# Differential attention with RG-LRU on one core: negated scaled scores, value scale in a copy, products re-placed

## The chip, the core and the metric

One core of a Trainium2 chip runs the kernel. The metric is device time in microseconds (us), the median of three runs: 497.36 us before (497.15 to 498.44). One further execution was taken with a profile. The engines have short names: PE (TensorE), DVE (VectorE), ACT (ScalarE), POOL (GpSimd), and SP, which issues most DMAs.

## The reference

A hybrid encoder layer on 16 meta rows and 1024 sequence rows of width 1024. One projection gives queries, keys, values, a gate and the two inputs of a linear recurrence (RG-LRU). The part that the change touches is differential attention: four heads, each with two score maps whose softmaxes are subtracted.

```
scores = einsum('bqhmd,bkhmd->bhmqk', qb, kb) * scale
scores = where(mask, scores, -inf)          # chunk-causal, 64 rows a chunk
p = softmax(scores, axis=-1)
w = p[:, :, 0] - lam * p[:, :, 1]
o = einsum('bhqk,bkhd->bqhd', w, vb)
...
o = rms_norm(o, subln_w, SUBLN_EPS) * (1.0 - lam_init)
att_out = o * silu(g_att)
lru_out = rg_lru(conv(x_lru)) * silu(g_lru)
out = rms_norm(h + concat(att_out, lru_out) @ w_out, final_norm_w)[16:]
```

## The kernel before

Nearly all products are split into a high and a low half and done as three passes. The first part (up to about 250 us) projects the sequence, gate by gate, and runs the recurrence on the other engines. What follows, from the first score to the end, is the attention with everything that can be pushed beneath it; the change lies there.

**Tiles and steps.** The 1024 query rows make eight tiles of 128, worked in the order 3, 7, 6, 5, 4, 2, 1, 0 (tile i sees the first 16 + 128(i+1) keys, so the work of a step differs). `order` has 32 steps, one for each tile and head. `attend()` writes the instructions of a step in program order:

1. `transposes` of the weights of the step three back (PE into PSUM, ACT copies out as `wT`);
2. `scores(i, h, 0)`, the first map;
3. waiting products (`at_least`) up to two thirds of the step's number in the table `MF`, with `combine` of the step before between them;
4. `transposes` of the low half, then `scores(i, h, 1)`, the second map, then the rest of the step's `MF` products;
5. `halve` of the step before, and `weigh`: the product with the values (`O`) of the step three back.

The "waiting products" are a list (`fill`): first the value projection (`psv`), then for each tile the product of the recurrence's result with the output weights (`psol`, four pieces of six matmuls a tile), later that of the attention's result (`psoa`). `MF[s]` says how many pieces step s places; a piece is six 512-wide matmuls. Its sum is 88.

**One map** (`scores`). PE writes scores into `pss`. DVE adds the mask and takes the row maximum in one instruction (a custom operation and a short read of its accumulator, which gives `mx`). For tile 7, whose row is longer than 1024, the 16 meta columns are kept apart (`sme`, `m2`), so DVE also takes the larger of `mx` and `m2`, a `TENSOR_TENSOR` of 128x1. ACT then makes the bias from the maximum, `mx*nesc + lnsw` (an `Identity` of 128x1), and next `Exp(esc*e + mx)` over the row with its sum. `esc` is the score scale of each row, `nesc` its negative; both are 128x1 operands.

**combine and halve.** DVE forms the ratio of the two sums (`rec`, then a `TENSOR_SCALAR` into `mx`), joins the two maps (`SCALAR_TENSOR_TENSOR e<-e,mx`), and splits the result into two fp16 halves (`w`). ACT does the first half for tiles 7 and 3. POOL copies the meta columns aside (`wm`).

**finish** (a chain of small steps for each tile, taken up whenever the planner's clock has moved on): ACT copies `O` to `o`, DVE scales `rec` by `isc[:, 2:3]` (the value scale), ACT squares and sums `o` by head (`sq`), DVE and POOL make the inverse root (`sums`, a power on POOL), POOL multiplies `o` by the gate and by `rec`, and PE transposes `o` (`pa`) once the planner believes `o` to be ready. ACT copies `pa` to `af`, POOL splits that into `at`, and the tile's `psoa` pieces join the list.

**The planner.** `Clock` keeps a made-up time for each engine from a fixed cost per instruction; `tick` and `pace` hand out the background chains by it, so a change of a cost or of an instruction list moves where chains are written into the program. Among those chains is `load_wo`, which loads rows of the output weights (`woraw`, SP), copies the high half on ACT (`woh`) and subtracts on POOL (`wol`, 128x1024).

PSUM holds two score banks of 1024 columns (later narrower ones), three banks shared by products and transposes (`bank`), and one for `O`; a product waits until DVE or ACT has emptied the bank that it takes. Each engine's queue runs in order: an instruction that waits holds back all that stand behind it.

Of the kernel before, what the change touches and what calls it, by code (L numbers as in the profile page):

```python
# [12 lines left out]
AF = mybir.ActivationFunctionType  # L13
OP = mybir.AluOpType
AX = mybir.AxisListType
# [4 lines left out]
T = NM + S  # L20
# [10 lines left out]
NEG = -3.0e38  # L31
# [6 lines left out]
class Clock:  # L38
# [5 lines left out]
    def __init__(self):  # L44
        self.now = dict.fromkeys(self.RATE, 0.0)
        self.written, self.used, self.rings = {}, {}, {}

    def ready(self, *aps):
        return max([self.written.get(a.tensor.name, 0.0) for a in aps], default=0.0) + self.HOP
# [11 lines left out]
    def engine(self, key, eng):  # L61
        clock = self

        class Timed:
            def __getattr__(self, op):
                f = getattr(eng, op)

                def call(*a, **k):
                    aps = [x for x in list(a) + list(k.values()) if hasattr(x, "tensor")]
                    clock.step(key, op, aps)  # L70
                    return f(*a, **k)  # L71
                return call
        return Timed()

    def step(self, key, op, aps):
        fix, rate = self.RATE[key]
        out = aps[0]
        n = int(np.prod(out.shape[1:]))
        if key == "PE" and aps[-1].dtype == F32 and op == "matmul":
            rate *= 4  # L80
        if op == "tensor_copy" and key == "V":
            rate *= 0.55
        t = max(self.now[key], self.ready(*aps) if key != "PE" else
                max(self.written.get(x.tensor.name, 0.0) for x in aps))
        t += fix + n * rate
        self.now[key] = t
        for x in aps:
            self.used[x.tensor.name] = t
        self.written[out.tensor.name] = t
# [3 lines left out]
def hybrid_layer_kernel(ctx: ExitStack, tc: tile.TileContext, xT, x, meta, w6, nwT,  # L93
                        par, wg, lamv, subw, w_out, fnw, cosT, sinT, ident, sel, bmask, out):
    nc = tc.nc
    clock = Clock()
    V, A, G, PE = (clock.engine(k, e) for k, e in zip(("V", "A", "G", "PE"),
                                                      (nc.vector, nc.scalar, nc.gpsimd, nc.tensor)))
# [210 lines left out]
    for k in range(KC - 2):  # L309
# [16 lines left out]
        if k == 3:  # L326
# [20 lines left out]
            e = cst([P, NB], name="spe")  # L347
# [62 lines left out]
    lnsw = cst([P, 1], name="lnsw")  # L410
# [51 lines left out]
    mask = cst([P, T], BF16, name="mask")  # L462
# [3 lines left out]
    isc = cst([P, 3], name="isc")  # L466
# [315 lines left out]
    esc = cst([P, 1], name="esc")  # L782
# [70 lines left out]
    def begin(i):  # L853
        n = NM + P * (i + 1)
        d = st[i] = dict(n=n, k0=NM if n > 1024 else 0,
                         sm=cst([P, 2, NH], name=f"sums{i}"), mx=cst([P, 2, NH], name=f"mx{i}"),
                         rec=cst([P, 2, NH], name=f"rec{i}"),
                         wm=const.tile([P, 2, NH, NM], F16, tag="wm", bufs=3, name="wm"),
                         e={}, w={}, wT={})
        if d["k0"]:  # L860
            pm = bank([P, NMAP, NM], name="pssm")
            q = QT[i]
            for m in range(NMAP):
                PE.matmul(pm[:, m, :], q[:, 0, m, :], K[m][:, 0:NM], start=True, stop=False)
                PE.matmul(pm[:, m, :], q[:, 1, m, :], K[m][:, 0:NM], start=False, stop=True)
            sme = slot("raw", [P, NMAP, NM], name="sme")
            V.tensor_copy(sme, pm)
            m2 = cst([P, NMAP], name="m2")
            V.tensor_reduce(m2, sme, axis=AX.X, op=OP.max)
            d["sme"], d["m2"] = sme, m2  # L870

    def scores(i, h, a):

        d = st[i]
        n, k0, q, m = d["n"], d["k0"], QT[i], 2 * h + a
        ps = score_banks()
        for j in range(2):
            for s0 in range(0, n - k0, 512):
                s1 = min(s0 + 512, n - k0)
                PE.matmul(ps[:, s0:s1], q[:, j, m, :], K[m][:, k0 + s0:k0 + s1], start=(j == 0), stop=(j == 1))  # L880
        e = slot("work", [P, T], name="e")
        mx = d["mx"][:, a, h:h + 1]
        V.tensor_tensor_reduce(out=e[:, k0:n], in0=ps[:, 0:n - k0], in1=mask[:, T - n + k0:],
                               op0=OP.add, op1=OP.max, scale=1.0, scalar=NEG, accum_out=mx)
        if k0:
            A.copy(e[:, 0:NM], d["sme"][:, m, :])
            V.tensor_tensor(mx, mx, d["m2"][:, m:m + 1], op=OP.max)
        A.activation(mx, mx, AF.Identity, scale=nesc, bias=lnsw)
        A.activation(e[:, 0:n], e[:, 0:n], AF.Exp, scale=esc, bias=mx, accum_out=d["sm"][:, a, h:h + 1])
        d["e"][h, a] = e  # L890

    def combine(i, h):
# [65 lines left out]
    def finish(i):  # L958

        d = st[i]  # L960
        O = d["O"]
        r0 = d["rec"][:, 0, :]
        V.tensor_scalar(r0, r0, isc[:, 2:3], None, op0=OP.mult)
        g = slot("raw", [P, NH, P], name="gate")
        dma(g, ga_d[i].rearrange("p (h d) -> p h d", h=NH))
        o = slot("raw", [P, NH, P], name="o")
        A.copy(o.rearrange("p h d -> p (h d)"), O)
        yield
        so = d["sm"][:, 0, :]
        sq = const.tile([P, P], BF16, tag="sq", bufs=1, name="sq")  # L970
        for h in range(NH):
            A.activation(sq, o[:, h, :], AF.Square, scale=r0[:, h:h + 1], accum_out=so[:, h:h + 1])
        yield
        yield
        V.tensor_scalar(so, so, 1.0 / P, SUBLN_EPS, op0=OP.mult, op1=OP.add)
        G.tensor_tensor(so, so, pw[:, 0:NH], op=OP.pow)
        yield
        yield
        G.tensor_tensor(r0, r0, so, op=OP.mult)
        G.tensor_tensor(o, o, g, op=OP.mult)  # L980
        G.tensor_tensor(o, o, r0.unsqueeze(2).to_broadcast([P, NH, P]), op=OP.mult)
        yield
        while fill and clock.ready(o) > clock.now["PE"] + 0.3:
            yield
        pa = bank([P, NH, P], name="pa")
        for h in range(NH):
            PE.transpose(pa[:, h, :], o[:, h, :], idf)
        at = d["at"] = slot("work", [P, 2, NH, P], F32R, name="at")
        backlog.append(i)
        af = slot("raw", [P, NH, P], name="af")  # L990
        A.activation(af, pa, AF.Copy, scale=sw8)
        G.tensor_copy(at[:, 0], af)
        G.tensor_tensor(at[:, 1], af, at[:, 0].bitcast(F32), op=OP.subtract)
        while i not in res_done or len(in_proj) >= 3:
            yield
        in_proj.append(i)
        d["xr"] = slot("work", [P, D], name="res")
        dma(d["xr"], res_d[i])
        while fill and clock.ready(at, d["xr"]) > clock.now["PE"] + 0.3:
            yield  # L1000
        fill.append(out_att(i))
# [138 lines left out]

    filled = [0]

    MF = [6, 7, 10, 4, 3, 4, 5, 4, 3, 1, 2, 2, 1, 1, 0, 2, 1, 2, 1, 2, 1, 2, 2, 2, 1, 2, 1, 2, 1, 3, 1, 3, 2, 3, 0, 1]

    def at_least(n):
        while fill and filled[0] < n:
# [36 lines left out]
    def attend():  # L1183

        TL = 3

        def trans(hl):
            if tra:
# [135 lines left out]
```

## Time and profile before

| | before |
|---|---|
| median of three runs | 497.36 us (497.15 to 498.44) |
| profiled execution, its own time | 498.2 us |
| its span, first to last instruction | 496.4 us |
| mean granted PE clock | 0.993 |
| PE / PE weight loads busy | 470.6 (95%) / 376.9 (76%) |
| DVE / ACT / POOL busy | 369.6 (74%) / 321.5 (65%) / 128.0 (26%) |
| DMA engines, mean | 138 GB/s |

The profile names instructions by what they write and read, `out<-in`. All engine calls pass through one helper, so most rows carry its line, L71; the tile names tell them apart. A row of the timeline has start, duration (both us), engine, operation, shapes, count, and in brackets the engine's idle time just ahead of it with what ended it. [...] The grouped rows have count, busy time in total and mean ns of one, then the idle time ahead of them.

### The profile page before, as it was taken

How to read it: one execution, taken by the hardware profiler on the slowest of the kernel's cores; microseconds unless marked ns; L12 is line 12 of the kernel's file. 1: busy time of each engine (PE TensorE's matmuls, PEld its weight loads, DVE VectorE, ACT ScalarE, POOL GpSimd, SP SyncE). 2: the span in 40 equal slices, each digit the busy share in tenths (PEclk: the TensorE clock that was granted, in tenths of full speed). 3: DMA queues.
4: the chain of work that ended last, by engine and by line, in shares of the span. 5: the costliest groups of instructions: out<-in, count | busy, mean ns of one | idle time of the engine just before them, and what ended most of it. 6: DMA issues, size and time to landing. Idle time of an engine off the chain costs nothing.

```text
span 496.4 us, 7797 instructions
## 1 busy us (share of the span) xinstructions
PE 470.6 (95%) x2844; PEld 376.9 (76%) x2844; DVE 369.6 (74%) x626; ACT 321.5 (65%) x624; POOL 128.0 (26%) x171
## 2 busy tenths in 40 slices
PE   6999999999999999999999999898898999999994
PEld 5996989988888888888776677576676778776773
DVE  5656987596798758954663666899889898888543
ACT  5787433563628657513663668698789888897733
POOL 0103202201101000000010242157333424364782
PEclk9999999999999999999999999999899999999998
DMA  7993221252132123278550136684643475505433
GB/s 223 384 404 122 86 85 44 64 166 70 28 79 70 38 88 124 85 259 266 177 182 31 44 86 168 172 233 150 163 115 110 105 190 159 140 0 192 162 115 127
DMA packets 50151, 68.33 MB, mean 138 GB/s; under 512 B 21009, under 2 KB 30129, under 8 KB 50113
## 3 DMA queue, kind: packets, MB, share of 16 engines
q1 hardware_dynamic: 38240, 55.21, 33.9%
q0 software_dynamic: 11872, 12.63, 10.5%
q8 instruction: 22, 0.36, 0.3%
q14 instruction: 17, 0.13, 0.1%
HBM read 48.91 MB, written 18.91 MB: 137 GB/s over the span
## 4 chain that ended last, share of the span: by engine, by line
PE 71%; DVE 13%; ACT 7%; issue 4%; DMA 2%; POOL 2%; SPq 0%; POOLq 0%; ACTq 0%; DVEq 0%
PE pss L71 39%; PE psv L71 6%; DVE e L71 6%; PE ps L71 6%; PE psx L71 5%; PE psol L71 5%; DVE w L71 3%; PE psg L71 2%; PE O L71 2%; ACT e L71 2%; PE psoa L71 2%; PE pt L71 2%; DVE mx L71 2%; POOL o L71 1%; ACT mx L71 1%
## 5 line engine op out<-in xcount | busy, mean ns | idle before, releaser
L71 PE MATMUL pss<-xs,w 128*128 128x512 f32 (+1 forms) x720 | 142.4, 345 | 4.2 <-ACT xs L71 4.2
L71 PEld LDWEIGHTS pss<-xs,w 128*128 128x128 f32 x720 | 120.5, 190 | 24.4 <-ACT xs L71 4.2
L71 ACT ACTIVATE e<-e,mx,esc 128x528 f32<-128x528 f32 (+7 forms) x64 | 56.4, 882 | 2.5
L71 DVE CUSTOM_DVE_ANT_0 e<-pss,mask 128x528 f32<-128x528 f32 (+7 forms) x64 | 49.1, 766 | 10.4 <-PE pss L71 10.2
L71 PE MATMUL psv<-w,xs 128*128 128x512 f32 x192 | 48.9, 404 | 0.8 <-DVE v L71 0.8
L71 PE MATMUL psol<-woh,lr 128*128 128x512 f32 x128 | 42.7, 414 | 3.5 <-DVE v L71 2.2
L71 PE MATMUL pss<-w,xs 128*128 128x512 f32 x192 | 46.0, 394 | 0.0
L71 ACT ACTIVATE mx<-mx,lnsw,nesc 128x1 f32<-128x1 f32 x64 | 24.7, 386 | 32.5 <-DVE mx L71 32.2
L71 PE MATMUL pss<-kst,qt 128*128 128x512 f16 (+3 forms) x208 | 43.5, 322 | 0.5 <-DVE mx L71 0.5
L71 PEld LDWEIGHTS psv<-w,xs 128*128 128x128 f32 x192 | 35.3, 188 | 10.7 <-DVE v L71 1.2
L71 PE MATMUL psoa<-woh,at 128*128 128x512 f32 (+1 forms) x136 | 41.9, 391 | 0.9 <-ACT psoa L71 0.9
L71 DVE TENSOR_TENSOR w<-wraw,w 128x512 fp32r<-128x512 f32 (+2 forms) x49 | 31.7, 669 | 14.5 <-ACT w L71 14.3
L71 PEld LDWEIGHTS pss<-w,xs 128*128 128x128 f32 x192 | 35.7, 188 | 7.9
L71 ACT COPY wT<-pt 128x1024 f16<-128x1024 f16 (+5 forms) x48 | 37.7, 786 | 0.6 <-PE pt L71 0.6
L71 DVE SCALAR_TENSOR_TENSOR e<-e,mx 128x528 f32<-128x528 f32 (+7 forms) x32 | 36.2, 1130 | 1.1
L71 ACT ACTIVATE w<-wraw 128x512 fp32r<-128x512 f32 x47 | 28.6, 620 | 9.2 <-DMA wraw<-in_w_dram 8.7
L71 PE MATMUL ps<-xs,w 128*128 128x512 f32 x120 | 34.4, 394 | 0.0
L71 PEld LDWEIGHTS psol<-woh,lr 128*128 128x128 f32 x128 | 23.3, 190 | 10.5 <-DVE v L71 2.6
L71 DVE TENSOR_TENSOR w<-e,w 128x528 f16<-128x528 f32 (+7 forms) x32 | 29.6, 925 | 0.8
L71 PEld LDWEIGHTS <-wT 128*128 128x128 f16 x432 | 25.9, 98 | 5.0 <-issue 2.2
L71 PE MATMUL O<-v,wT 128*128 128x128 f16 x432 | 29.4, 219 | 0.0
L71 PEld LDWEIGHTS psoa<-woh,at 128*128 128x128 f32 x136 | 23.8, 188 | 6.1 <-ACT psoa L71 2.3
(198 smaller groups left out, 858.7 us busy)
## 6 DMA issues: line engine op xcount, KB each, us to landing
wraw<-in_w_dram SPq DMA_DIRECT2D x47, 256.0 KB, 3.7
xt<-in_x_dram SPq DMA_DIRECT2D x8, 512.0 KB, 7.0
woraw<-in_w_out_dram SPq DMA_DIRECT2D x8, 512.0 KB, 4.2
xres<-in_x_dram SPq DMA_DIRECT2D x8, 512.0 KB, 4.2
lr<-lru_d POOLq DMA_DIRECT2D x8, 512.0 KB, 5.5
res_d<-xres SPq DMA_DIRECT2D x8, 512.0 KB, 2.9
res<-res_d SPq DMA_DIRECT2D x8, 512.0 KB, 4.1
out_dram<-res SPq DMA_DIRECT2D x7, 512.0 KB, 2.9
```

Source lines behind the costliest of these rows:

```text
L71: return f(*a, **k)
```

## The change

- `scores`: the custom operation now also multiplies by `nesc` and takes the minimum instead of the maximum, so `e` and `mx` hold negated, scaled scores. For tile 7 the minimum starts from `m2` (then a minimum over `sme`, written scaled), which replaces the separate 128x1 `TENSOR_TENSOR`. The copy of the meta columns is written ahead of it.
- The exponential takes -1.0 as an immediate scale in place of the 128x1 operand `esc`, and `mx` as its bias.
- The `Identity` that makes the bias remains for the first map only, where it adds `lnsw`, without `nesc`. For the second map it is gone: its factor cancels in the ratio of the sums.
- `finish`: the scaling of `rec` by `isc` is gone; the copy of `O` to `o` does it, as an activation with a 128x1 scale.
- The planner's clock, from `attend` on, adds 0.4 + 0.15 per column for a power and 0.19 for an ACT instruction with an accumulator.
- The table `MF` has other numbers (sum 87).

```diff
     def __init__(self):
         self.now = dict.fromkeys(self.RATE, 0.0)
         self.written, self.used, self.rings = {}, {}, {}
+        self.fine = False
...
-                    clock.step(key, op, aps)
+                    more = 0.0
+                    if clock.fine and k.get("op") == OP.pow:
+                        more = 0.4 + 0.15 * aps[0].shape[-1]
+                    if clock.fine and key == "A" and k.get("accum_out") is not None:
+                        more = 0.19
+                    clock.step(key, op, aps, more)
...
-    def step(self, key, op, aps):
+    def step(self, key, op, aps, more=0.0):
...
-        t += fix + n * rate
+        t += fix + n * rate + more
...
             sme = slot("raw", [P, NMAP, NM], name="sme")
-            V.tensor_copy(sme, pm)
+            V.tensor_scalar(sme, pm, nesc, None, op0=OP.mult)
             m2 = cst([P, NMAP], name="m2")
-            V.tensor_reduce(m2, sme, axis=AX.X, op=OP.max)
+            V.tensor_reduce(m2, sme, axis=AX.X, op=OP.min)
...
-        V.tensor_tensor_reduce(out=e[:, k0:n], in0=ps[:, 0:n - k0], in1=mask[:, T - n + k0:],
-                               op0=OP.add, op1=OP.max, scale=1.0, scalar=NEG, accum_out=mx)
         if k0:
             A.copy(e[:, 0:NM], d["sme"][:, m, :])
-            V.tensor_tensor(mx, mx, d["m2"][:, m:m + 1], op=OP.max)
-        A.activation(mx, mx, AF.Identity, scale=nesc, bias=lnsw)
-        A.activation(e[:, 0:n], e[:, 0:n], AF.Exp, scale=esc, bias=mx, accum_out=d["sm"][:, a, h:h + 1])
+        V.tensor_tensor_reduce(out=e[:, k0:n], in0=ps[:, 0:n - k0], in1=mask[:, T - n + k0:], op0=OP.add, op1=OP.min,
+                               scale=nesc, scalar=d["m2"][:, m:m + 1] if k0 else -NEG, accum_out=mx)
+        if a == 0:
+            A.activation(mx, mx, AF.Identity, bias=lnsw)
+        A.activation(e[:, 0:n], e[:, 0:n], AF.Exp, scale=-1.0, bias=mx, accum_out=d["sm"][:, a, h:h + 1])
...
         r0 = d["rec"][:, 0, :]
-        V.tensor_scalar(r0, r0, isc[:, 2:3], None, op0=OP.mult)
...
-        A.copy(o.rearrange("p h d -> p (h d)"), O)
+        A.activation(o.rearrange("p h d -> p (h d)"), O, AF.Copy, scale=isc[:, 2:3])
...
-    MF = [6, 7, 10, 4, 3, 4, 5, 4, 3, 1, 2, 2, 1, 1, 0, 2, 1, 2, 1, 2, 1, 2, 2, 2, 1, 2, 1, 2, 1, 3, 1, 3, 2, 3, 0, 1]
+    MF = [8, 5, 10, 5, 2, 5, 5, 4, 1, 3, 3, 0, 1, 1, 0, 2, 1, 2, 3, 0, 1, 2, 2, 0, 2, 3, 1, 2, 1, 3, 1, 3, 2, 3, 0, 0]
...
         TL = 3
+        clock.fine = True
```

How the instructions stand now, at three places. Numbers in names are buffer numbers, and helper rows are L71 before and L77 after.

**DVE, one head of tile 7 (step 5: its second head).** `ISA e,mx` is the custom operation on a map and `ISA mx` its accumulator read; `v` is the low half of a value tile. Before:

```order
L71 ISA e,mx_2512<-pss,mask 128x1024
L71 ISA mx_2512 128x1
L71 TENSOR_TENSOR mx_2512<-mx_2512,m_2534 128x1
L71 RECIPROCAL rec_2513<-sums_2511 128x2
L71 TENSOR_SCALAR mx_2512<-rec_2513,nlam,sums_2511 128x1
L71 SCALAR_TENSOR_TENSOR e<-e,mx_2512 128x1040
L71 ISA e,mx_2512<-pss,mask 128x1024
L71 ISA mx_2512 128x1
L71 TENSOR_TENSOR mx_2512<-mx_2512,m_2534 128x1
L71 SCALAR_TENSOR_TENSOR v<-psv,rsv,v 128x512
L71 TENSOR_TENSOR w_2654<-e,w_2654 128x1040
```

After:

```order
L77 ISA e,mx_2517<-pss,mask,m_2539,nesc 128x1024
L77 ISA mx_2517 128x1
L77 RECIPROCAL rec_2518<-sums_2516 128x2
L77 TENSOR_SCALAR mx_2517<-rec_2518,nlam,sums_2516 128x1
L77 SCALAR_TENSOR_TENSOR e<-e,mx_2517 128x1040
L77 SCALAR_TENSOR_TENSOR v<-psv,rsv,v 128x512
L77 ISA e,mx_2517<-pss,mask,m_2539,nesc 128x1024
L77 ISA mx_2517 128x1
L77 TENSOR_TENSOR w_2646<-e,w_2646 128x1040
```

The two `TENSOR_TENSOR` of `mx` are gone, the custom operation reads `m` and `nesc` as well, and the value tile now stands ahead of the second map where it stood behind it.

**POOL, between the first psol products and the finishing of tile 3 (steps 6 to 10).** `sums` by `pw` is the power of tile 3; the two `o` rows behind it make what PE transposes. Before:

```order
L71 TENSOR_TENSOR wol<-woraw,woh 128x1024
L71 COPY wm<-w_2831 128x2x16
L1034 DMA lr<-lru_d 128x8x128
L71 TENSOR_TENSOR wol<-woraw,woh 128x1024
L71 TENSOR_TENSOR sums_2183<-sums_2183,pw 128x4
L71 TENSOR_TENSOR wol<-woraw,woh 128x1024
L71 TENSOR_TENSOR rec_2185<-rec_2185,sums_2183 128x4
L71 TENSOR_TENSOR o<-o,gate 128x512
L71 TENSOR_TENSOR o<-o,rec_2185 128x512
L71 COPY wm<-w_2946 128x2x16
L71 TENSOR_TENSOR wol<-woraw,woh 128x1024
```

After:

```order
L77 COPY wm<-w_2729 128x2x16
L77 TENSOR_TENSOR wol<-woraw,woh 128x1024 x3
L1040 DMA lr<-lru_d 128x8x128
L77 COPY wm<-w_2836 128x2x16
L77 TENSOR_TENSOR wol<-woraw,woh 128x1024
L77 COPY wm<-w_2946 128x2x16
L77 TENSOR_TENSOR sums_2183<-sums_2183,pw 128x4
L77 TENSOR_TENSOR rec_2185<-rec_2185,sums_2183 128x4
L77 TENSOR_TENSOR o<-o,gate 128x512
L77 TENSOR_TENSOR o<-o,rec_2185 128x512
```

The four `wol` subtractions of the second half of the output weights (the first of them stands just above the rows of before) have drawn together: three stand one behind the other, the fourth follows one `wm` later, and none is left between the power and the two `o` rows. The power itself stands behind the `wm` of one head more (`w_2946` is tile 7's last head in both).

**PE, where tile 3's `o` is transposed (`pa`).** Before, in step 10 behind the product with the values and the transposed meta weights:

```order
L71 MATMUL O<-v,wT 128x128
L71 LDWEIGHTS wm
L71 MATMUL ptm<-idh,wm 128x128
L71 MATMUL pa<-idf,o 128x128 x4
L71 LDWEIGHTS w_3052
L71 MATMUL pt<-idh,w_3052 128x128
```

After, in step 10 between the two products that follow the first map:

```order
L77 MATMUL pss<-kst,qt 128x400
L77 MATMUL psol<-woh,lr 128x512 x2
L77 MATMUL psol<-wol,lr 128x512
L77 MATMUL psol<-woh,lr 128x512 x2
L77 MATMUL psol<-wol,lr 128x512
L77 MATMUL pa<-idf,o 128x128 x4
L77 MATMUL psol<-woh,lr 128x512 x2
L77 MATMUL psol<-wol,lr 128x512
L77 MATMUL psol<-woh,lr 128x512 x2
L77 MATMUL psol<-wol,lr 128x512
```

The transposes of `o` stand one map and one product with the values earlier. Step 8 places one `psol` piece where it placed three, steps 9 and 10 three each where they placed one and two, and step 11 none where it placed two. Later, `pa` of tile 6 moves from step 17 to step 18, and that of tile 4 from the end of step 26 to behind its first map; those of tiles 7 and 5 stay.

## The prediction

> **What bounds the kernel now.** I read the page's busy shares and its chain first, then busy time by stretch from the first steps of tile 7 on, then what PE waits for.
>
> ```profile
> PE 470.6 (95%) x2844; PEld 376.9 (76%) x2844; DVE 369.6 (74%) x626; ACT 321.5 (65%) x624; POOL 128.0 (26%) x171
> ...
> PE 71%; DVE 13%; ACT 7%; issue 4%; DMA 2%; POOL 2%; SPq 0%; POOLq 0%; ACTq 0%; DVEq 0%
> ```
>
> ```profile
> 284.00:325.80 41.80, 39.38 (x260) 28.66 (x259) 30.82 (x50) 29.86 (x53) 13.45 (x12) 1.00 0.51 133
> 325.80:358.70 32.90, 29.04 (x248) 22.35 (x246) 30.52 (x44) 27.59 (x49) 18.22 (x16) 0.95 0.66 185
> 358.70:404.50 45.80, 42.03 (x400) 32.54 (x398) 41.80 (x83) 40.60 (x88) 17.04 (x23) 1.00 0.52 141
> 404.50:458.40 53.90, 51.68 (x393) 40.29 (x391) 46.38 (x132) 47.25 (x136) 23.99 (x36) 1.00 0.41 117
> 458.40:489.00 30.60, 29.33 (x148) 22.81 (x148) 16.09 (x34) 16.94 (x49) 22.41 (x25) 1.00 0.39 137
> 489.00:496.40 7.40, 0.86 (x8) 0.66 (x6) 1.81 (x4) 1.90 (x6) 0.92 (x3) 0.75 0.36 142
> ```
>
> The columns are the stretch, its length, the busy time of PE, PEld, DVE, ACT and POOL, PE's granted clock, DMA share and GB/s. The matmuls are the same before and after, so a gain can only come out of PE's idle time (length less PE busy): 2.42, 3.86, 3.77, 2.22 and 1.27 us, 13.5 in all; the last 7.4 us are the final norm behind the last matmul, which the change doesn't touch. In the second and third stretch DVE is busy 93% and 91%, ACT 84% and 89%: there PE, DVE and ACT run neck and neck. What PE waits for says the same:
>
> ```profile
> PE pa L71 <- DVE xres L71: 3.4, 1, 3.4
> PE pa L71 <- POOL o L71: 2.5, 4, 1.1
> PE psol L71 <- DVE v L71: 2.2, 1, 2.2
> PE pt L71 <- ACT wT L71: 1.4, 3, 0.6
> PE psol L71 <- ACT wT L71: 1.1, 1, 1.1
> ```
>
> Total, times, longest: two single waits on DVE, some small ones on ACT, and four on the chain that makes `o`.
>
> **The change part by part.** *ACT.* The rows that price it:
>
> ```profile
> L71 ACT ACTIVATE mx<-mx,lnsw,nesc 128x1 f32<-128x1 f32 x64 | 24.7, 386 | 32.5 <-DVE mx L71 32.2
> L71 ACT ACTIVATE v<-psv,rsv 128x512 f16<-128x512 f32 x8 | 5.3, 681 | 3.2 <-PE psv L71 2.2 <-DVE rsv L71 0.9
> L71 ACT COPY o<-O 128x512 f32<-128x512 f32 x8 | 4.6, 569 | 0.0
> ```
>
> ```profile
> 297.36 0.39 ACT L71 ACTIVATE mx<-mx,lnsw,nesc 128x1 f32<-128x1 f32 x1 [1.91 <-DVE mx L71]
> 297.78 1.26 ACT L71 ACTIVATE e<-e,mx,esc 128x1040 f32<-128x1040 f32 x1
> ```
>
> 32 of the 64 `mx` instructions go: 32 x 0.386 = 12.4 us. The copy of `O` and the value copy have one shape and differ by one 128x1 operand: 681 - 569 = 112 ns for it. 64 exponentials lose such an operand (7.2) and the other 32 `mx` too (3.6), eight copies of `O` gain one (0.9). ACT loses 22.3 us. On the path of a second map 0.42 us goes (start of `mx` to start of `e`), of a pair of maps 0.42 + 3 x 0.11 = 0.75.
>
> *DVE.*
>
> ```profile
> L71 DVE TENSOR_SCALAR mx<-rec,nlam,sums 128x1 f32<-128x1 f32 x32 | 8.7, 273 | 1.2
> L71 DVE TENSOR_SCALAR f<-f 128x1 f32<-128x1 f32 x1 | 0.2, 153 | 0.0
> L71 DVE TENSOR_TENSOR mx<-mx,m 128x1 f32<-128x1 f32 x8 | 5.8, 723 | 0.3
> L71 DVE TENSOR_SCALAR rec<-rec,isc 128x4 f32<-128x4 f32 x8 | 3.2, 404 | 0.0
> L71 DVE CUSTOM_DVE_ANT_0 e<-pss,mask 128x912 f32<-128x912 f32 x8 | 8.8, 1101 | 1.3 <-PE pss L71 1.3
> ```
>
> Two operands of 128x1 cost 273 - 153 = 120 ns, one 60. No row shows the custom operation with such an operand. It moves no more elements, so I see no gain and take 0 below; above, 0.12 each (as though one cost what two cost here); I take 0.06, the step of the nearest rows. 64 times for `nesc` and 8 for tile 7's start value: 4.3 us (0 to 8.6). Removed: 5.8 + 3.2 = 9.0 us. DVE stands at -4.7, but much of the 5.8 is one operation held up, as the next part shows. The scaled copy `sme` is one instruction with one operand more, 0.06.
>
> *284 to 325.8: tile 7 beside the value products.*
>
> ```profile
> 301.02 1.22 DVE L71 CUSTOM_DVE_ANT_0 e<-pss,mask 128x1024 f32<-128x1024 f32 x1
> ...
> 302.28 1.57 DVE L71 TENSOR_TENSOR mx<-mx,m 128x1 f32<-128x1 f32 x1
> ...
> 309.32 0.75 DVE L71 SCALAR_TENSOR_TENSOR v<-psv,rsv,v 128x512 f16<-128x512 f32 x1 [2.41 <-ACT v L71]
> ...
> 311.13 1.22 DVE L71 CUSTOM_DVE_ANT_0 e<-pss,mask 128x1024 f32<-128x1024 f32 x1
> ```
>
> ```profile
> 305.12 1.03 PE L71 MATMUL pss<-kst,qt 128*128 128x512 f16 x4
> ...
> 313.62 1.03 PE L71 MATMUL pss<-kst,qt 128*128 128x512 f16 x4
> 316.80 0.73 PE L71 MATMUL psol<-woh,lr 128*128 128x512 f32 x2 [2.15 <-DVE v L71]
> ```
>
> DVE takes 10.11 us for a head (301.02 to 311.13), PE 8.50 (305.12 to 313.62); PE runs ahead until the first `psol` finds its bank full and waits 2.15. Of DVE's head 1.57 is the 128x1 maximum, which is removed, and 2.41 is waiting for ACT's value copy, which stood behind bias and exponential of the second map. Now the value tile stands ahead of that map. What it still waits for, the first map's exponential, ACT's copy of `w` and the value copy, I put at 1.5. 10.11 - 1.5 - 0.9 + 4 x 0.06 = 7.95, under PE's 8.50: PE becomes the bound and its wait goes. **-2.0** (0 to -2.42). What is late next is PE itself.
>
> *325.8 to 358.7: tile 6.*
>
> ```profile
> 338.25 2.35 POOL L71 TENSOR_TENSOR wol<-woraw,woh 128x1024 fp32r<-128x1024 f32 x1 [3.11 <-ACT woh L71]
> ...
> 342.96 1.31 POOL L71 TENSOR_TENSOR o<-o,rec 128x512 f32<-128x512 f32 x1
> ...
> 345.27 2.39 POOL L71 TENSOR_TENSOR wol<-woraw,woh 128x1024 fp32r<-128x1024 f32 x1
> ```
>
> ```profile
> 338.28 3.29 DVE L71 SCALAR_TENSOR_TENSOR e<-e,mx 128x912 f32<-128x912 f32 x1
> ...
> 343.41 1.83 DVE L71 TENSOR_TENSOR w<-e,w 128x912 f16<-128x912 f32 x1
> ...
> 346.69 1.94 DVE L71 SCALAR_TENSOR_TENSOR e<-e,mx 128x912 f32<-128x912 f32 x1
> ...
> 350.83 1.11 DVE L71 TENSOR_TENSOR w<-e,w 128x912 f16<-128x912 f32 x1
> ...
> 360.99 1.17 DVE L71 SCALAR_TENSOR_TENSOR e<-e,mx 128x912 f32<-128x912 f32 x1
> ```
>
> ```profile
> 349.28 1.11 PE L71 MATMUL pa<-idf,o 128*128 128x128 f32 x4 [3.36 <-DVE xres L71]
> ...
> 368.97 0.66 PE L71 MATMUL pa<-idf,o 128*128 128x128 f32 x4 [1.12 <-POOL o L71]
> ```
>
> The same operations take 1.17 and 1.11 us where POOL is quiet, and 3.29, 1.83 and 1.94 beside `wol` and the `o` rows: 3.6 us lost, and PE's 3.36 is DVE arriving that late. Behind the wait PE also runs slower (the same four transposes 1.11 against 0.66 us; granted clock 0.95 over the stretch). The change draws `wol` together into steps 7 and 8, ahead of this stretch's end, and the chain of `o` no longer has one in it: `o` was ready at 344.27, and without that `wol` (2.35) and the wait before it (3.11), but with the power one `w` later (about 1.2), it is ready near 340, about when PE now asks for it. That the copies `woh` and the loads behind them come a step earlier costs ACT nothing new, and SP's later `qt` load is for step 12. The price of the move: DVE meets the same `wol` earlier. Between 0 and 3.6 of it comes back; I take half, 1.8. Step 8 keeps PE busy with one `psol` piece instead of three and step 11 with none, so PE runs out of cover there: +0.7 (0 to 2.2), booked apart. Eight custom operations add 0.5. So -3.86 (all idle time of the stretch) - 0.8 (half of the clock's 5% of 32.9) + 1.8 + 0.5 = **-2.4** (+1.5 to -5.5).
>
> [...]
>
> *358.7 to 404.5: tiles 5 and 4.* Eight heads take 8 x 0.75 = 6.0 from ACT (40.60 to 34.6 of 45.8), and 16 custom operations add 1.0 to DVE's 41.80: DVE remains, with 3 us of room. The waits for `wT` (1.4 and 1.1 in the list, partly here) go; those for `o` halve, since squares and copy come earlier. **-1.8** (+0.5 to -3.7).
>
> *404.5 to 458.4.* ACT is the busiest helper (47.25 of 53.9) and loses 12 x 0.75 = 9.0. The waits are scattered; I take half of 2.22: **-1.1** (0 to -2.2). *458.4 on:* **-0.2**. *Fill pieces:* **+0.7**.
>
> The sum is -2.0 - 2.4 - 1.8 - 1.1 - 0.2 + 0.7 = -6.8 us. The profiled execution took 498.2 us, 1.8 beyond its span of 496.4, and stands 0.84 above the median; by its own measure it would come to 491.4. From the median, 497.36 - 6.8 = **490.6**.
>
> **The rivals.**
>
> *PE is full anyway.* At 95% busy little can come back; the small waits only change places, and DVE pays its 4.3 us. For it: each wait is short. Against: the two long waits (3.4 and 2.2) have a cause each that the change moves. It would give the 2.0 of the first stretch less the 1.5 that 24 custom operations cost between 325 and 404: 496.9. [...]
>
> *The wol burst (slower).* Place: steps 7 and 8. If every `wol` shuts one two-input DVE operation out by the 2.12 seen at 338.28, four cost 8.5 instead of 3.6, +4.9, at a place where PE has one piece of cover. DVE stays late through tiles 6 to 4, so the gains of both stretches (2.4 and 1.8) are lost. 497.36 - 2.0 - 1.1 - 0.2 + 0.7 + 4.9 = 499.7. It is slower than before once the burst costs over 2.6, and by over 0.3% from 4.1 on. Against: at 338.28 the operation ran as soon as that `wol` ended although POOL had more to do, so the two take turns; and three of the copies `woh` that feed the burst take ACT time, which spreads it.
>
> *All waits go.* With nothing left but PE: 497.36 - 13.5 = 483.9.
>
> *The change does not do what it says:* if the planner puts `pa` where `o` is late again, PE stands there with the next maps behind it. Tile 3's is asked for a map and a product earlier; its 3.36 would stay in full, 494.0. This lies in the forecast's range.
>
> **How the numbers follow.** Forecast, 485 to 495: 0.60. PE full, 495 to 498.8: 0.16, of which 0.04 is still faster. Slower, by the burst or a dearer custom operation, 498.9 to 502: 0.17. All waits go: 0.07. A measurement of this kernel tells about 0.3%, 1.5 us, from no change. Faster 0.60 + 0.04 + 0.07 = 0.71, the same 0.12, slower 0.17. The range runs from 484.5 to 498.8, which leaves out the slower cases and little below.
>
> **What would show it.** Right: no wait over 1 us at the first `psol` and at tile 3's `pa`; 32 `mx` rows on ACT, exponentials 0.11 shorter; the custom operation of 912 columns 0.06 longer than its 1.10; ACT busy near 299. Wrong: `SCALAR_TENSOR_TENSOR e` rows over 3 us around steps 7 and 8 with PE idle behind them (the burst); PE idle between 325 and 404 unchanged (PE full, or DVE the bound); a wait on POOL's `o` over 2 us at tile 3's `pa`.

## The result, and the profile after

The changed kernel takes **486.32 us** (median of four runs, 486.07 to 486.99) against 497.8 for the kernel before, measured beside it: a ratio of 0.9772 with a 95% interval of 0.9753 to 0.979, 2.3% faster. The profiled execution took 486.57 us with a span of 484.8, and 498.2 with 496.4 before. The forecast was 490.6: right in sign, 4.3 us too small.

The page of the changed kernel, busy times and the chain that ended last by engine:

```profile
PE 466.2 (96%) x2844; PEld 375.4 (77%) x2844; DVE 364.3 (75%) x610; ACT 303.3 (63%) x592; POOL 126.1 (26%) x171
...
PE 87%; DVE 5%; ACT 3%; issue 2%; DMA 1%; POOL 0%; POOLq 0%; ACTq 0%; SPq 0%
```

PE's share of the chain went from 71% to 87%. What PE waits for in the changed kernel (total, times, longest; the 4.3 us are at the very start, in both kernels):

```profile
PE pss L77 <- ACT xs L77: 4.3, 1, 4.3
PE psol L77 <- ACT wT L77: 1.9, 3, 1.0
PE pa L77 <- POOL o L77: 1.5, 1, 1.5
PE O L77 <- ACT wT L77: 1.3, 1, 1.3
PE pt L77 <- ACT wT L77: 0.7, 1, 0.7
```

Both long waits on DVE are gone, and of the four for `o` one is left (1.5 us; the longest was 1.1). To see where, one needs borders at the same piece of work. I take the first score product of tile 6, of tile 5 and of tile 2, the last score product, and the end of the last matmul. Between them both tables place the same pieces, but for one `psol` piece of six matmuls (about 1.4 us) that before does beside tile 6 and the changed kernel beside tile 7, with one `psv` piece moved ahead of tile 7 in its place. Busy time by stretch with these borders, columns as in the prediction; before:

```profile
285.00:325.82 40.82, 38.40 (x256) 27.86 (x255) 29.84 (x50) 28.86 (x51) 12.47 (x11) 1.00 0.52 136
325.82:358.70 32.88, 29.02 (x248) 22.33 (x245) 30.50 (x44) 27.59 (x49) 18.20 (x16) 0.95 0.66 185
358.70:403.56 44.86, 41.09 (x395) 31.75 (x393) 40.89 (x81) 39.70 (x86) 17.04 (x23) 1.00 0.50 138
403.56:452.69 49.13, 47.16 (x370) 37.32 (x368) 41.71 (x119) 43.14 (x122) 21.32 (x32) 1.00 0.41 111
452.69:489.86 37.17, 35.65 (x183) 27.23 (x182) 21.66 (x49) 22.72 (x66) 25.10 (x29) 1.00 0.40 142
```

And after:

```profile
285.00:323.05 38.05, 38.05 (x257) 28.16 (x256) 29.07 (x44) 29.46 (x52) 16.95 (x12) 1.00 0.59 170
323.05:349.68 26.63, 26.06 (x241) 19.91 (x239) 24.58 (x37) 21.53 (x41) 13.25 (x14) 1.00 0.76 201
349.68:395.34 45.66, 41.18 (x395) 31.67 (x393) 42.88 (x82) 36.55 (x80) 15.94 (x23) 1.00 0.51 135
395.34:442.28 46.94, 46.59 (x367) 37.13 (x367) 42.99 (x120) 38.79 (x117) 22.10 (x33) 1.00 0.40 113
442.28:478.24 35.96, 34.51 (x184) 27.75 (x183) 18.33 (x43) 20.43 (x59) 23.91 (x28) 1.00 0.42 147
```

Tile 7 is 2.8 us shorter, tile 6 6.3 (4.9 for equal work), tiles 5 and 4 are 0.8 **longer**, tiles 2 to 0 are 2.2 shorter and what follows the last score 1.2. The same borders serve for all runs below (us, from each run's trace; the first column starts at tile 7's first score product):

| run | tile 7 | tile 6 | 5 and 4 | 2 to 0 | behind the last score | median |
|---|---|---|---|---|---|---|
| before | 36.24 | 32.88 | 44.87 | 49.13 | 37.17 | 497.5 |
| new arithmetic alone (e1) | 33.27 | 29.41 | 43.21 | 46.85 | 45.02 | 495.81 |
| arithmetic, powers (e2) | 33.27 | 29.42 | 44.13 | 46.95 | 38.84 | 490.75 |
| arithmetic, table (e3) | 33.26 | 26.66 | 45.00 | 48.32 | 39.73 | 492.40 |
| table, powers (e4) | 35.29 | 29.66 | 46.36 | 47.25 | 40.06 | 496.52 |
| all three: the changed kernel | 33.26 | 26.63 | 45.66 | 46.94 | 35.95 | 486.32 |
| ACT heavy (e5) | 33.81 | 28.03 | 46.46 | 48.44 | 35.97 | 490.42 |
| minimum apart (e6) | 35.24 | 27.52 | 45.63 | 46.93 | 36.02 | 489.63 |
| e1, later norm (e7) | 33.27 | 29.42 | 43.20 | 46.85 | 40.49 | 491.65 |
| before without four wol (e8) | 36.23 | 29.01 | 44.84 | 49.13 | 37.21 | 494.03 |
| powers, no accumulators (e9) | 33.26 | 26.34 | 45.04 | 46.83 | 37.08 | 486.82 |
| after without wol (e10) | 33.28 | 25.91 | 45.64 | 46.89 | 36.04 | 485.93 |
| e6 without wol (e11) | 33.28 | 26.48 | 45.65 | 46.89 | 36.03 | 486.53 |
| pa of tile 7 later (e12) | 33.26 | 26.65 | 47.42 | 46.99 | 36.73 | 489.53 |

The kernel before took 497.4 to 497.6 us in the three sets of runs. Ratios to it and their intervals: e1 0.9951 (0.9934 to 0.9968), e2 0.9864 (0.9844 to 0.9884), e3 0.9888 (0.987 to 0.9906), e4 0.9979 (0.9965 to 0.9993).

### The profile page after: what moved, and what is told of

The parts are those of the page before. It is cut to its first block, busy times and chain, and to the rows that moved or that the text cites. A ratio compares the mean times of both kernels' runs of the same rounds, so it can differ in the third digit from the quotient of the medians.

```text
span 484.8 us, 7748 instructions
## 1 busy us (share of the span) xinstructions
PE 466.2 (96%) x2844; PEld 375.4 (77%) x2844; DVE 364.3 (75%) x610; ACT 303.3 (63%) x592; POOL 126.1 (26%) x171
## 4 chain that ended last, share of the span: by engine, by line
PE 87%; DVE 5%; ACT 3%; issue 2%; DMA 1%; POOL 0%; POOLq 0%; ACTq 0%; SPq 0%
PE pss L77 42%; PE psv L77 9%; PE psol L77 7%; PE psoa L77 7%; PE ps L77 6%; PE psx L77 5%; PE O L77 4%; DVE e L77 3%; PE psg L77 2%; PE pt L77 2%; DMA res<-res_d 1%; DVE w L77 1%; PE psmr L77 1%; PE pa L77 1%; ACT wT L77 1%
## 5 line engine op out<-in xcount | busy, mean ns | idle before, releaser
L77 PE MATMUL pss<-xs,w 128*128 128x512 f32 (+1 forms) x720 | 142.4, 345 | 4.3 <-ACT xs L77 4.3
L77 PEld LDWEIGHTS pss<-xs,w 128*128 128x128 f32 x720 | 120.4, 190 | 24.5 <-ACT xs L77 4.3
L77 ACT ACTIVATE e<-e,mx 128x528 f32<-128x528 f32 (+7 forms) x64 | 50.5, 790 | 27.4 <-DVE mx L77 26.1
L77 PE MATMUL psv<-w,xs 128*128 128x512 f32 x192 | 48.4, 402 | 0.2 <-DVE v L77 0.2
L77 DVE CUSTOM_DVE_ANT_0 e<-pss,mask,nesc 128x528 f32<-128x528 f32 (+6 forms) x56 | 42.6, 761 | 7.7 <-PE pss L77 6.5
L77 PE MATMUL pss<-w,xs 128*128 128x512 f32 x192 | 46.0, 394 | 0.0
L77 PE MATMUL psol<-woh,lr 128*128 128x512 f32 x128 | 42.8, 415 | 1.9 <-ACT wT L77 1.9
L77 DVE TENSOR_TENSOR w<-wraw,w 128x512 fp32r<-128x512 f32 (+2 forms) x49 | 31.7, 669 | 16.2 <-ACT w L77 16.0
L77 PE MATMUL pss<-kst,qt 128*128 128x512 f16 (+3 forms) x208 | 42.6, 318 | 0.7 <-DVE mx L77 0.7
L77 PEld LDWEIGHTS psv<-w,xs 128*128 128x128 f32 x192 | 35.3, 188 | 10.0 <-issue 0.8
L77 PEld LDWEIGHTS pss<-w,xs 128*128 128x128 f32 x192 | 35.7, 188 | 7.9
L77 PE MATMUL psoa<-woh,at 128*128 128x512 f32 (+1 forms) x136 | 41.6, 389 | 0.2 <-ACT psoa L77 0.2
L77 ACT COPY wT<-pt 128x1024 f16<-128x1024 f16 (+5 forms) x48 | 37.6, 784 | 1.0 <-PE pt L77 0.8
L77 DVE SCALAR_TENSOR_TENSOR e<-e,mx 128x528 f32<-128x528 f32 (+7 forms) x32 | 35.0, 1095 | 1.1
L77 ACT ACTIVATE w<-wraw 128x512 fp32r<-128x512 f32 x47 | 28.5, 619 | 9.7 <-DMA wraw<-in_w_dram 9.2
L77 PE MATMUL ps<-xs,w 128*128 128x512 f32 x120 | 34.4, 394 | 0.0
L77 PEld LDWEIGHTS <-wT 128*128 128x128 f16 x432 | 25.6, 98 | 6.6 <-issue 2.7
L77 PE MATMUL O<-v,wT 128*128 128x128 f16 x432 | 29.4, 219 | 1.3 <-ACT wT L77 1.3
L77 DVE TENSOR_TENSOR w<-e,w 128x528 f16<-128x528 f32 (+7 forms) x32 | 28.9, 904 | 0.9
L77 PEld LDWEIGHTS psol<-woh,lr 128*128 128x128 f32 x128 | 22.9, 188 | 8.6 <-ACT wT L77 3.2
L77 DVE RECIPROCAL a<-a 128x208 f32<-128x208 f32 x20 | 27.8, 1423 | 0.0
L77 PEld LDWEIGHTS psoa<-woh,at 128*128 128x128 f32 x136 | 24.1, 188 | 4.5 <-ACT psoa L77 0.4
```

## The experiments

### The three parts alone (e1 to e4)

The change has three parts: the arithmetic, the table `MF`, and the powers (with ACT's accumulators) in the planner's clock. Each run puts some of them back:

```diff
# e1: the changed kernel with
-    MF = [8, 5, 10, 5, 2, 5, 5, 4, 1, ...
+    MF = [6, 7, 10, 4, 3, 4, 5, 4, 3, ...
-        clock.fine = True
+        clock.fine = False
# e2: only the old MF put back; e3: only clock.fine = False
# e4: new MF and clock.fine = True, the lines of scores, begin and finish as before
```

> The changed arithmetic with the old table MF and without counted powers; PE's order is nearly that of before. Theory P (placement: the table took away the long waits at the first psol and at tile 3's pa): both waits stay, over 1 and over 2 us, only the scattered waits for ACT shrink: 3 to 5 us under the kernel before, 6 to 8 over the changed one. Theory A (arithmetic: a lighter ACT and DVE took them away): both waits are gone or under 1 us, 8 to 11 us under the kernel before. Theory S (neither alone, they need one another): under 2.5 us gained.

> As the run before it, with powers counted in the planner's clock; still the old table. By P and by A the counted powers are worth little here: within 1 us of the run before it. If counting the powers is what put pa behind a finished o, the wait at tile 3's pa is gone and it is 2.5 us or more faster than the run before it.

> The changed kernel without counted powers (new arithmetic and new table). By P and by A: within 1 us of the changed kernel, which is 11.2 us under before. If the counted powers matter, pa waits for POOL's o by 1 to 3 us in sum and it is 1.5 us or more slower than the changed kernel.

> The arithmetic of before with the new table and with counted powers; PE's order is nearly that of the changed kernel. P: the psol wait under 1 us and the pa wait of tile 3 under 1.5 us, 6 to 8 us under the kernel before. A: ACT and DVE are as late as before, the long waits stay or move, gain 0 to 3 us. S: under 2.5 us, and the sum of this gain and that of the first run stays 5 us or more below 11.2.

The arithmetic alone gains 1.7 us, table and powers alone 1.0, all together 11.2. That is theory S by its numbers, and it says that they need one another. The stages say more. Up to the last score the arithmetic alone has taken 10.4 us away (36.24 + 32.88 + 44.87 + 49.13 = 163.12 against 152.74), and both long waits with it: in its trace `psol` has no wait on DVE and tile 3's `pa` none at all, although its `MF` is the old one. (1.1 us of waiting on DVE's `xres` is left, at transposes in tile 6.) Its `wol` rows still stand on POOL beside tile 6, but its joins there take 1.30, 1.26 and 1.17 us: none starts behind a `wol`, and a `wol` that starts within a join (at 330.41) takes 2.83 us, the one ahead of it 2.41. How much of that is the lighter engines and how much the luck of the moment, no run here tells apart. So theory A holds for the two waits, and P falls: the new places without the arithmetic (e4) gain 1.0 us, not 6 to 8. Then 7.85 us are lost again behind the last score: 4.7 are idle time of PE (6.2 against 1.5), and much of the rest is the granted clock, 0.92 over this stretch of e1 where before had 1.00:

```profile
442.43:487.45 45.02, 38.84 (x184) 29.71 (x183) 20.90 (x43) 20.31 (x57) 24.32 (x29) 0.92 0.36 129
```

Counting the powers brings 6.2 of these back (45.02 to 38.84), and the table another 2.9. My expectation of e2, that powers are worth under 1 us, was wrong by a factor of five, and not for the reason of its other case, since tile 3's `pa` waits in neither run. In e3 `pa` waits 1.1 us for `o`, which is little of the 6.1 us that it loses to the changed kernel.

What goes wrong there in e1 shows on DVE. `res<-res,s,fn` is the final norm of a finished tile, `s` the power that POOL makes for it. DVE, POOL and PE in e1, idle time in brackets:

```profile
441.48 0.15 DVE L77 TENSOR_SCALAR s<-s 128x1 f32<-128x1 f32 x1
445.45 1.42 DVE L77 SCALAR_TENSOR_TENSOR res<-res,s,fn 128x512 f32<-128x512 f32 x2 [3.81 <-POOL s L77]
...
447.57 0.68 DVE L77 TENSOR_TENSOR res<-res,psoa 128x512 f32<-128x512 f32 x1
```

```profile
442.94 0.61 POOL L77 CAST at<-af 128x512 fp32r<-128x512 f32 x1 [1.58 <-ACT af L77]
443.64 1.27 POOL L77 TENSOR_TENSOR at<-af,at 128x512 fp32r<-128x512 f32 x1
444.87 0.55 POOL L77 TENSOR_TENSOR s<-s,pw 128x1 f32<-128x1 f32 x1
```

```profile
449.06 0.73 PE L77 MATMUL psoa<-woh,at 128*128 128x512 f32 x2 [2.65 <-ACT psoa L77]
```

The power is ready at 445.42, because it stands on POOL behind `at`, which waited for ACT. DVE has reached its consumer at 441.6 and stands still for 3.81 us with nothing wrong in its own work. Behind it in the queue is `res<-res,psoa`, which empties a bank of `psoa`; ACT squares that result, and PE waits 2.65 us for the bank. The row that PE's wait names (ACT) is two steps away from the cause. With the lighter arithmetic alone the planner had written these rows so: the power behind `at` on POOL, and its consumer right behind `s` on DVE, where the kernel before had other work of DVE between the two (`s` ends at 451.56, the consumer starts at 452.99 without a wait).

### The final norm written later (e7)

To test that reading, e1 was run again with only the place of this consumer altered:

```diff
         G.tensor_tensor(t, t, pw[:, 0:1], op=OP.pow)
-        yield
+        for _ in range(4):
+            yield
```

> The first run again (new arithmetic, old table, no counted powers), with one thing altered: the final norm of a tile writes its multiplication four planner steps behind POOL's power, not one, so that DVE's res<-res,s,fn stands behind the next res<-res,psoa. Theory N (that run lost its gain behind the last score because DVE stood waiting for the power, 3.8 and 3.2 us, with psoa's emptying queued behind it): the stretch from the last score to the last matmul falls from 45.0 to 38 to 42 us and the time to 490 to 493. Rival (the tail is long because PE's order there is bad, or POOL is late): within 1.5 us of the first run's 495.8.

491.65 us, 4.2 less than e1, and the last stretch falls from 45.02 to 40.49, while the other four are the same to 0.01. DVE in e7 meets a finished power:

```profile
447.36 1.41 DVE L77 SCALAR_TENSOR_TENSOR res<-res,s,fn 128x512 f32<-128x512 f32 x2
461.23 1.41 DVE L77 SCALAR_TENSOR_TENSOR res<-res,s,fn 128x512 f32<-128x512 f32 x2
```

Theory N is shown: what e1 loses behind the last score is, for the larger part (4.5 of 7.85 us), a consumer at the head of an in-order queue. Of the 4.5, 2.2 are idle time of PE; much of the rest is the clock, 0.96 over this stretch in e7. What is left over e2 (40.49 against 38.84) is 0.5 us of idle time (e7 waits 3.1 us for POOL's `at`, e2 3.5 for ACT's `psoa`) and 1.1 of busy time at a lower clock (0.96 against 0.99).

The counted powers undo the same wait from its other end. In e2 the consumer still stands right behind `s` on DVE, as in e1. But the power stands ahead of `at` on POOL, for tiles 7 and 5 in e2, e9 and the changed kernel alike, and the consumer there waits 0.7 us or less. In e3, without them, both powers stand behind `at`, and at tile 5 DVE waits 4.44 us. POOL in the changed kernel, tile 7:

```profile
441.27 0.55 POOL L77 TENSOR_TENSOR s<-s,pw 128x1 f32<-128x1 f32 x1
443.04 0.70 POOL L77 CAST at<-af 128x512 fp32r<-128x512 f32 x1 [1.22 <-ACT af L77]
```

### Which half of the planner's clock (e9)

```diff
-                        more = 0.19
+                        more = 0.0
```

> The changed kernel with the planner's clock counting the powers but not the 0.19 for ACT's accumulators. Theory N (what matters is that the planner knows when a power is done): within 1 us of the changed kernel's 486.3. Rival (the extra time on ACT is what sets the chains right): 489 to 492, with DVE standing before POOL's s for over 3 us as in the run without counted powers.

486.82, within 0.5 us of the changed kernel: the powers are what counts.

### ACT as heavy as before (e5)

```diff
         if a == 0:
             A.activation(mx, mx, AF.Identity, bias=lnsw)
-        A.activation(..., AF.Exp, scale=-1.0, bias=mx, ...)
+        else:
+            nc.scalar.activation(mx, mx, AF.Identity, scale=one1, bias=lnsw)
+        A.activation(..., AF.Exp, scale=neg1, bias=mx, ...)
```

(`one1` and `neg1` are 128x1 constants; the added instruction is not told to the planner, so that the order stays.)

> The changed kernel with the instructions of every engine in the same order, but ACT as heavy as before: a bias instruction again ahead of the second map's exponential (32 of about 0.39 us) and a 128x1 scale operand in all 64 exponentials (0.09 each): 18 us more of ACT. Theory A1 (ACT's relief carries the gain to the last score): 492 to 496, about what the run with the arithmetic of before and the new placement took (496.5), waits for ACT's wT come back. Theory A2 (DVE's relief carries it): within 1.5 us of the changed kernel.

490.42: 4.1 us for 16.0 us more of ACT (319.3 us busy against 303.3; 18 were expected), between the two theories. Every stage up to the last score loses 0.55 to 1.5, the stretch behind it nothing. ACT's relief is worth about a quarter of itself, spread over many small waits, and is not the whole gain.

### What the wol rows cost before (e8) and after (e10)

```diff
-            G.tensor_tensor(l, r, h.bitcast(F32), op=OP.subtract)
+            clock.step("G", "tensor_tensor", [l, r, h.bitcast(F32)])
+            wo[k] = (h, h)
# e8: in before, for rows 0 to 3 alone; e10: in after, for all eight
```

In both the products take the high half in place of `wol`, so this part of the result is left out.

> The kernel before in the same order, without the four subtractions wol of the second half of the output weights (their products take the high half in its place, so this part of the result is left out). Lock theory (the wol rows beside it stretch DVE's joins to 3.0, 3.3 and 1.9 us and thereby make the 3.4 us wait at tile 3's pa): the joins take 1.2 to 1.4 us there, the pa wait is under 1 us, 3 to 5 us under the kernel before. Rival (the wait comes from where pa stands, behind a bank that DVE empties late anyway): the joins shorten, but the wait stays over 2 us and less than 1.5 us is gained.

> The changed kernel in the same order without all eight subtractions wol (the products take the high half, so that part of the result is left out). If the locks that are left in the changed kernel (joins of 2.3, 3.2 and 2.2 us) still cost PE time: 1.5 us or more under 486.3. If PE's cover hides them, as its 1.0 us of idle time between 324 and 357 says: within 1 us.

e8 gains 3.5 us, 3.87 in the stage of tile 6 and nothing elsewhere. Its joins and its `pa` of tile 3, where before had 3.04, 3.29 and 1.94 us and a wait of 3.36:

```profile
327.94 1.30 DVE L71 SCALAR_TENSOR_TENSOR e<-e,mx 128x1040 f32<-128x1040 f32 x1
337.22 1.33 DVE L71 SCALAR_TENSOR_TENSOR e<-e,mx 128x912 f32<-128x912 f32 x1
343.52 1.17 DVE L71 SCALAR_TENSOR_TENSOR e<-e,mx 128x912 f32<-128x912 f32 x1
...
345.35 0.66 PE L71 MATMUL pa<-idf,o 128*128 128x128 f32 x4 [0.49 <-DVE xres L71]
```

And the stage of tile 6 by its busy times:

```profile
325.42:354.44 29.02, 27.64 (x248) 21.09 (x246) 23.46 (x42) 26.99 (x49) 10.68 (x12) 1.00 0.72 210
```

The lock theory holds, that the joins are stretched beside `wol` and that PE's wait follows from it; by what means `wol` holds a join up, no run shows. The granted clock of the stage (third figure from the end) is 1.00 again without the wait, where before had 0.95. e10 shows that the `wol` rows that the changed kernel still has cost it 0.4 us, too little to be told from nothing. Yet they still stretch DVE's joins there, once as much as before (the first two below, 2.29 and 3.23 us, take 1.30 each in e10; the third takes 2.19 in e10 too, and here stands beside POOL's `o<-o,gate`):

```profile
317.31 2.29 DVE L77 SCALAR_TENSOR_TENSOR e<-e,mx 128x1040 f32<-128x1040 f32 x1
326.50 3.23 DVE L77 SCALAR_TENSOR_TENSOR e<-e,mx 128x1040 f32<-128x1040 f32 x1
333.68 2.19 DVE L77 SCALAR_TENSOR_TENSOR e<-e,mx 128x912 f32<-128x912 f32 x1
...
339.19 0.60 PE L77 MATMUL pa<-idf,o 128*128 128x128 f32 x4
```

DVE now has the slack to be late by 2 us, and PE, with `psol` pieces on both sides of `pa`, does not notice.

### Tile 7's minimum apart (e6), and without wol (e11)

```diff
-                               scale=nesc, scalar=d["m2"][:, m:m + 1] if k0 else -NEG, accum_out=mx)
+                               scale=nesc, scalar=-NEG, accum_out=mx)
+        if k0:
+            nc.vector.tensor_tensor(mx, mx, d["m2"][:, m:m + 1], op=OP.min)
# e11: this, and the edit of e10
```

> The changed kernel in the same order, but the smaller of the two minima of tile 7 is again an instruction of its own on DVE (8 of 0.72 us, less 8 x 0.06). A2: DVE is late again beside the value products, the wait at the first psol comes back with 1.5 us or more, 488.3 to 489.5. A1: no wait there, within 0.7 us of the changed kernel.

> The kernel with tile 7's minimum apart (489.6), again without the eight wol. If its 3.3 us came from joins that its later DVE puts beside a wol (one of 3.5 us in its trace), it comes within 0.8 us of the run without wol ahead of it. If the eight small instructions cost by themselves (their own time and the later bias), it stays 2.5 us or more above that run.

e6 loses 3.3 us, 2.0 of them beside tile 7, which looks like A2's price for eight small instructions. Its rows say otherwise. DVE first, then POOL:

```profile
292.87 1.26 DVE L895 TENSOR_TENSOR mx<-mx,m 128x1 f32<-128x1 f32 x1
...
298.88 0.16 DVE L895 TENSOR_TENSOR mx<-mx,m 128x1 f32<-128x1 f32 x1
...
301.49 3.49 DVE L77 SCALAR_TENSOR_TENSOR e<-e,mx 128x1040 f32<-128x1040 f32 x1
...
329.18 4.11 DVE L77 SCALAR_TENSOR_TENSOR e<-e,mx 128x1040 f32<-128x1040 f32 x1
```

```profile
291.72 2.40 POOL L77 TENSOR_TENSOR wol<-woraw,woh 128x1024 fp32r<-128x1024 f32 x1 [0.97 <-ACT woh L77]
301.46 2.42 POOL L77 TENSOR_TENSOR wol<-woraw,woh 128x1024 fp32r<-128x1024 f32 x1 [1.45 <-ACT woh L77]
...
329.81 2.37 POOL L77 TENSOR_TENSOR wol<-woraw,woh 128x1024 fp32r<-128x1024 f32 x1
```

Six of the eight take 0.16 us. But DVE's shift lays its join at 301.49 behind a `wol` that began 0.03 us earlier, and it takes 3.49 in place of 1.30. e11 settles it: without the `wol` rows, the eight instructions cost 0.6 us (486.53 against 485.93), not 3.3. The join at 329.18 is less plain than the one at 301.49: it began 0.63 us ahead of the last `wol` and ended 1.1 us behind it. Just ahead of that `wol` POOL issued the `lr` DMA and copied `wm`; what held the join first is not shown.

### A try at the longest wait left (e12)

```diff
-        while fill and clock.ready(o) > clock.now["PE"] + 0.3:
+        while fill and clock.ready(o) > clock.now["PE"] + (-1.2 if i == 7 else 0.3):
```

> The changed kernel with one number altered: the planner takes tile 7's o for ready 1.5 us later, so its transposes pa, which wait 1.5 us for POOL's o, stand one head later on PE (those of tile 5 and tile 1 move a little too). If the wait is simply uncovered: 484.8 to 485.5. If it comes back elsewhere (the next product waits for ACT's wT there, or psoa starts later): within 0.7 us of 486.3, or slower.

489.53 (487.49 to 490.03), 3.2 us slower: the rival. The 1.5 us wait is gone, but PE stands longer elsewhere (a row of its timeline), and the clock drops behind that (3.41 us ahead of the drop, and 3.41 behind its start):

```profile
368.43 0.50 PE L77 MATMUL pt<-idh,w 128*128 128x128 f16 x6 [2.55 <-ACT wT L77]
```

```profile
365.53:368.94 3.41, 0.86 (x13) 0.66 (x11) 3.34 (x8) 2.77 (x7) 0.00 (x0) 1.00 0.00 0
368.94:372.35 3.41, 3.41 (x10) 2.54 (x9) 3.30 (x7) 2.67 (x7) 2.66 (x3) 0.50 0.00 0
```

No run beat the changed kernel with its whole computation.

## Why the prediction was right in sign and too small

- **What bounds it.** Right in the main: PE's matmuls are the same, and its idle time (span less busy) fell by 7.2 us, from 25.8 to 18.6. But its busy time fell by 4.4 as well (470.6 to 466.2), where the forecast allowed 0.8, for the clock. The clock behind tile 3's wait makes 1.7 of that; the rest is spread over the stages and was not traced.
- **Prices.** The custom operation takes 0.06 more with one operand (912 columns: 1.101 to 1.162) and 0.12 more with two (1024 columns: 1.220 to 1.339), as put. An operand of 128x1 on ACT costs 92 ns on the exponentials (882 to 790), not 112; that makes some 2 of the 4 us by which ACT came out above the 299 that was put (303.3), and the rest is open. Two grouped rows, kept apart by shape, and one of the page:

```profile
L77 DVE CUSTOM_DVE_ANT_0 e<-pss,mask,m 128x1024 f32<-128x1024 f32 x8 | 10.7, 1339 | 0.5 <-PE pss L77 0.2
L77 DVE CUSTOM_DVE_ANT_0 e<-pss,mask,nesc 128x912 f32<-128x912 f32 x8 | 9.3, 1162 | 1.4 <-issue 1.1 <-PE pss L77 0.2
```

```profile
L77 ACT ACTIVATE e<-e,mx 128x528 f32<-128x528 f32 (+7 forms) x64 | 50.5, 790 | 27.4 <-DVE mx L77 26.1
```

- **Tile 7, -2.0; measured -2.8 to -3.0.** The mechanism held: a head takes DVE 7.87 us (start of the custom operation at 304.32 to 312.19) and the next 8.14 (to 320.33) where 7.95 was forecast, and PE never waits. Two reasons in it were weaker than put. The value tile's new place was not needed, since e1, with the old table, has the same 33.27. And the maximum itself costs little (e11, 0.6 us); its 0.72 us before was mostly time held up beside `wol` (1.61, 1.57 and 1.80 us at 295.71, 302.28 and 324.36, each begun within a `wol`; the other five took 0.16).
- **Tile 6, -2.4 and +0.7 for the fill pieces; measured -4.9 for equal work.** Two terms failed in size. The price of +1.8 for `wol` moved earlier is at most 0.7 (26.63 to 25.91 in e10), as PE's `psol` pieces cover it. The clock was put at -0.8 and gave back the whole 5% of 32.9, 1.7. The lost cover did not show here. In the row at 338.28, `wol`'s 2.35 and a plain run of 1.17 make 3.52, 0.23 more than the 3.29 measured, so it held roughly that the operation ran as soon as that `wol` ended.
- **Tiles 5 and 4, -1.8; measured +0.8.** This failed in sign, though not for its reason: the arithmetic does give 1.7 here (e1). The table takes 1.5 to 1.8 back (e2 to the changed kernel, e1 to e3): by the gaps between its matmuls, PE stands 0.7 us longer in e3 than in e1 at tile 7's `pa`, 0.4 longer at the transposes ahead of it, and 0.6 behind step 19, which lost both its pieces as step 11 did. Counting the powers takes another 0.7 to 0.9 here (e3 to the changed kernel, e1 to e2). What the table takes is the lost cover of the +0.7, in the stage behind the one where it was put, and more than twice its size.
- **404.5 to the end, -1.1 and -0.2; measured -2.2 and -1.2.** Tiles 2 to 0 have their 2.2 by the arithmetic already (46.85 in e1). The step that failed in kind: counted powers were taken for a shift of single rows and got no price of their own. They are worth 5 us (e1 to e2) to 6 (e3 to the changed kernel), because with the lighter arithmetic alone the planner writes POOL's power behind `at`, with its consumer at the head of DVE's queue. What was put at -0.2 is the small rest, -1.2, of two large effects: +7.9 by the arithmetic and -9.1 by powers and table.
- **The rivals.** The burst happened (a join of 3.23 us beside it) and decided nothing. That PE is full did not hold, nor that tile 3's `pa` would meet a late `o` (it does not wait). "All waits go", at 483.9, came nearer (2.4 us off) than the forecast, but by luck: over the five stretches 6.9 of 13.5 us of idle time are still there, and less busy time of PE made up for most of that. What a `wol` beside a join costs is measured in e6, e8 and e11: the first join of tile 7 takes 3.49 us behind a `wol` in e6 and 1.30 without one in e11, and the three joins of tile 6 that took 3.04, 3.29 and 1.94 in before take 1.30, 1.33 and 1.17 in e8.

What stays open: why the `psv` piece moved ahead of tile 7 (about 1.4 us) shows as only 0.2 us there (tile 7's first score product at 289.59 and 289.79). That time varies by 1.7 us among these runs, so it can't be told.

## What to carry to other kernels

When work is taken off an engine under a planner, ask what the planner will now write earlier, and whether each of those instructions has its input by then: a consumer at the head of an in-order queue cost as much here (4.2 us, the clock included) as 16 us saved on ACT gained (4.1). Price a small instruction by what it shifts beside the instructions of other engines, not by its own mean; the same eight cost 3.3 us with `wol` on POOL and 0.6 without. And add the parts of a change only after running them apart: 1.7 and 1.0 made 11.

## What the runs showed of the hardware that was not expected

Waiting cost PE twice here: behind some waits the granted clock was 0.50 for 3.41 us. In the clock records of these traces it is 1.00 or 0.50, and each stretch at 0.50 that ends ahead of the last matmul lasts 3.41 us; other values in the rows above are means over both. The 3.41 us ahead of such a stretch in before, e4, e1 and e7, for the first two with the stretch itself:

```profile
345.88:349.29 3.41, 0.05 (x2) 0.01 (x1) 3.34 (x7) 2.52 (x4) 3.41 (x3) 1.00 0.00 0
349.29:352.70 3.41, 3.41 (x16) 2.59 (x17) 2.62 (x4) 2.38 (x6) 0.52 (x2) 0.50 1.06 209
```

```profile
333.05:336.46 3.41, 1.47 (x13) 0.76 (x12) 2.92 (x6) 3.32 (x6) 2.69 (x5) 1.00 0.00 0
336.46:339.87 3.41, 3.22 (x9) 2.53 (x10) 3.41 (x5) 3.38 (x6) 1.45 (x2) 0.50 0.07 30
```

```profile
446.99:450.40 3.41, 1.34 (x6) 1.05 (x6) 3.27 (x11) 2.11 (x8) 1.32 (x2) 1.00 0.82 282
```

```profile
472.05:475.46 3.41, 0.55 (x2) 0.19 (x1) 1.00 (x3) 2.81 (x7) 2.91 (x3) 1.00 0.39 149
```

So here it is not the length of one wait that counts. e4 has no wait over 1.2 us here, but two (0.99 and 1.14) close together, and the clock halves; the wait of 2.15 us in before leaves it at 1.00. Cut these four traces and that of e12 into pieces of 3.41 us whose borders fall on the start of a half-clock stretch. In the pieces right ahead of the half clock PE is busy for 0.05 us (before), 1.34 and 1.60 (e1), 1.47 (e4), 0.55 (e7) and 0.86 (e12); the least busy piece between tile 7 and the last matmul that the half clock does not follow has 1.77 in before, and in e4, between 300 and 372 us, 1.91. What the clock does between 1.60 and 1.77 is not shown. The 2.15 us lie across a border of two pieces (at 315.16), and leave 2.90 and 1.77 us busy. Tile 3's `pa` wait of 3.36 us thus cost, by estimate, another 1.7 (half of the 3.41). How much a kernel loses by it is no fixed sum: e1's executions spread from 493.3 to 496.1 us, the two shortest at a mean clock of 0.997 and the others at 0.989 to 0.991, so the 4.2 us of e7, taken between medians, would be 1.7 to 1.9 against those two.
